# One TensorE-bound decoder trunk: S5 states computed straight from PSUM with one scan per component, and eight projections placed among the quarters of S5's outputs

## The chip, the cores and the metric

The kernel runs on one core of one Trainium2 chip. The metric is the device time of one execution in microseconds (us). Before the change it was 1204.95 us, the median of three runs (1203.24, 1204.95, 1210.08). The engines are named as in the profile: PE is TensorE (PEld its weight loads), DVE is VectorE, ACT is ScalarE, POOL is GpSimd, SP issues the DMAs.

## The reference

Two layers. Each is: half a SwiGLU feed-forward, a mixer, half a SwiGLU feed-forward, all behind RMSNorm, on 272 tokens of width 1024. The change lies in the mixer:

```python
proj = h @ w_in                      # q, k, v | dn_qkv | dn_z | dn_b, dn_a | s5_u
o_sb = rmsnorm(stick_breaking_attention(q, k, v))
o_dn = rmsnorm(gated_deltanet(dn_qkv, b, a)) * silu(z)
bu = einsum(u, b_bar)                # S5, complex, 32 groups x 64 states
states = scan(x_t = abar * x_{t-1} + bu_t)
y = gelu(real(einsum(states, c)) + d * u)
o_s5 = rmsnorm(y * sigmoid(y @ w_glu + b_glu))
out = concatenate(o_sb, o_dn, o_s5) @ w_out
```

## The kernel before

Activations stand transposed in SBUF (128 features of a block by 272 tokens). Each large product is made of three fp32r matmuls (`mm3`: high by high, high by low, low by high), so each weight tile of 128x1024 is first split: ACT rounds it (`wh`, L136) and DVE subtracts (`wl`, L139; six in each mixer go to POOL). A unit (`unit`) is one such tile and 24 matmuls `proj` into one PSUM bank, which DVE empties (L1362 for q, k, v and z).

The mixer of one layer computes in the order of `ORD`. `conv` makes the six blocks of the DeltaNet's qkv. `dn_gates` and `dn_inverse` make the inverse of the triangular matrix of the delta rule: a chain of seven pairs of small DVE steps (L1004, L1005), a transpose T (L1009), and then levels of small matmuls `px` and `py` with a DVE or ACT step between each two. `dn_rest` makes the DeltaNet's outputs.

S5 runs over chunks of four tokens, 68 chunks. Its 16 state pairs are taken as four quarters r of four pairs. `s5` copies u into the chunk layout U, makes the inputs `pinc` (W1 by U) of a quarter in two PSUM banks (real and imaginary part), which ACT copies to `s5z`; then it rotates them (four products with cos and sin, one sum, one difference), runs the scan of each pair and part (8 of 128x68 in a quarter), and rotates back. Two products and one difference of each rotation run on POOL. `s5_outputs` makes the four quarters of outputs `pY` (M0 by U, W2 by the states; 12 fp32 matmuls in a quarter, which the trace shows as 24) and takes their GELU on ACT. `glu` is the gate: `pglu`, tanh, products, and the rounding of the result. `sb` is the attention, from its scores `pz` to its outputs `pob`. `w_out_part` multiplies with the output weights, S5's rows (S) first.

The order on each engine is made by the framework's scheduler, from the priorities in the code (`first()` 4000 for the DeltaNet, `second()` 1500 for the outputs of S5 and the gate) and from the PSUM banks of a tag (two each). `pinc`, `dn_rest` and `pY` share tag b. On an engine, instructions run strictly in their order. An ACT table set (`phase`) stands ahead of the functions that use it.

Of the kernel before, what the change touches and what calls it, by code (L numbers as in the profile page):

```python
# [18 lines left out]
P = 128  # L19
# [21 lines left out]
ORD = "czsrqgbmn"  # L41
# [22 lines left out]
class Trunk:  # L64
    def __init__(self, ctx, tc, a, out):
# [13 lines left out]
        self.blocks = (0, 4)  # L79

# [61 lines left out]
    def mm3(self, p, wh, wl, xh, xl, first, last):  # L142
        mm = self.nc.tensor.matmul
        mm(p, wh, xh, start=first, stop=False)  # L144
        mm(p, wh, xl, start=False, stop=False)  # L145
        mm(p, wl, xh, start=False, stop=last)  # L146
# [126 lines left out]
    def load_params(self, prm):  # L273
# [282 lines left out]
    def s5_alloc(self):  # L556
# [8 lines left out]
        self.dec = c.tile([P, NQ], F32, name="dec")  # L565
# [4 lines left out]
    def s5_tables(self, l, tmp):  # L570
# [17 lines left out]
        pin = tmp.tile([NQ, 3, P], F32, name="pin")  # L588
# [69 lines left out]
        tt(ci, t, rd, ALU.mult)  # L658
        tt(t, e1, e1, ALU.mult)
        tt(self.dec, t, t, ALU.mult)  # L660
# [3 lines left out]
        V.tensor_scalar(r4h, r4, 6144.0, 6144.0, op0=ALU.add, op1=ALU.subtract)  # L664
        tt(r4l, r4, r4h, ALU.subtract)
# [84 lines left out]
        for b in range(2):  # L750
# [20 lines left out]
            for h in range(2):  # L771
# [8 lines left out]
                R0 = tmp.tile([32, 4, P], F32, tag="R0", name="R0", bufs=1)  # L780
# [11 lines left out]
    def s5_tile(self, nm):  # L792
        return self.tmp.tile([P, 4, NCH], F32, tag="s5w", name=nm, bufs=4)

    def s5(self, u):
# [5 lines left out]
        for r in range(4):  # L801
            for j in range(4):
                o = U[32 * (3 - j):32 * (3 - j) + 32, r]
                i = u[32 * r:32 * r + 32].rearrange("p b (c j) -> p b c j", j=4)[:, :, :, j]
                (V.tensor_copy if j % 2 else A.copy)(o, i)  # L805
        self.S = []
        for r in range(4):
            z = []
            for o in range(2):
                p = self.psum("b", "pinc")  # L810
                for b in range(4):
                    PE.matmul(p[:, b * NCH:(b + 1) * NCH], self.W1[o][:, 4 * b + r, :], U[:, r, b, :], start=True, stop=True)
                t = tmp.tile([P, 4, NCH], F32, name=f"s5z{r}{o}")
                A.copy(t, p[:, :T].rearrange("p (b c) -> p b c", b=4))
                z.append(t)
            self.S.append(z)
        for r, z in enumerate(self.S):
            cs, sn = self.cs[:, r::4], self.sn[:, r::4]
            w = [tl("w") for _ in range(4)]
            V.tensor_tensor(w[0], z[0], cs, op=ALU.mult)  # L820
            G.tensor_tensor(w[1], z[1], sn, op=ALU.mult)
            V.tensor_tensor(w[2], z[1], cs, op=ALU.mult)
            V.tensor_tensor(w[3], z[0], sn, op=ALU.mult)
            V.tensor_tensor(z[0], w[0], w[1], op=ALU.add)
            G.tensor_tensor(z[1], w[2], w[3], op=ALU.subtract)
# [14 lines left out]
    def s5_outputs(self, u):  # L840

        A, PE = self.nc.scalar, self.nc.tensor
        for r in range(4):
            p = self.psum("b", "pY")
            for b in range(4):
                q = 4 * b + r
                po = p[:, b * NCH:(b + 1) * NCH]
                PE.matmul(po, self.M0[:, q, :], self.U[:, r, b, :], start=True, stop=False)  # L848
                for k in range(2):
                    PE.matmul(po, self.W2[k][:, q].rearrange("p k g c -> p (k g c)"), self.S[r][k][:, b, :], start=False, stop=k == 1)  # L850
            for t in range(4):
                o = u[32 * r:32 * r + 32].rearrange("p b (c t) -> p b c t", t=4)[:, :, :, t]
                self.act(o, p[32 * t:32 * t + 32, :T].rearrange("p (b c) -> p b c", b=4), AF.Gelu_apprx_tanh)
# [20 lines left out]
    def dn_products(self, rhs, nm, tag):  # L874
# [3 lines left out]
        t, tt = self.dn_tile([P, 8, P], nm), self.dn_tile([P, 32], nm + "t")  # L878
# [13 lines left out]
        return t, tt  # L892

    def dn_gates(self, l, qkv, ba):
# [71 lines left out]
        self.LT, self.LTt = self.dn_products(kb, "LT", "d")  # L966
# [105 lines left out]
    def dn_rest(self, qkv):  # L1072
# [20 lines left out]
        AT, ATt = self.dn_products(qn, "AT", "b")  # L1093
# [88 lines left out]
    def dn_out(self, zg, slot):  # L1182
# [6 lines left out]
        for b in range(2):  # L1189
# [8 lines left out]
            A.activation(self.xh[:, slot + b, :], y, AF.Copy)  # L1198
# [294 lines left out]
```

## Time and profile before

| | |
|---|---|
| median of three runs | 1204.95 us |
| profiled execution, and its span | 1212.91 us, 1211.1 us |
| PE busy | 1172.0 us (97%), mean granted clock 0.955 |
| DVE busy | 866.0 us (72%) |
| ACT busy | 626.1 us (52%) |
| POOL busy | 212.0 us (18%) |

[...] The mixer of layer 0 stands at about 230 to 425 us of the span, that of layer 1 at about 830 to 1030 us.

### The profile page before, as it was taken

The numbers are of one execution on the slowest core, as the hardware profiler recorded it, in microseconds if no ns is written. First come the engines' busy times: TensorE is split into PE (matmuls) and PEld (weight loads), VectorE is DVE, ScalarE is ACT, GpSimd is POOL, SyncE is SP. The second block draws the span as 40 slices with busy tenths as digits, with TensorE's granted clock in tenths as the row PEclk, the third lists the DMA queues.
The fourth block names the chain that finished last, engine by engine and source line by source line (L and its number), as shares of the span: only waits on it lengthen the run. The fifth ranks groups of instructions, "written<-read, shape, count | busy, mean of one in ns | idle before, by whom it ended". The sixth has DMA issues, their size and how long they took to land.

```text
span 1211.1 us, 23894 instructions
## 1 busy us (share of the span) xinstructions
PE 1172.0 (97%) x9544; PEld 1124.1 (93%) x9544; DVE 866.0 (72%) x1680; ACT 626.1 (52%) x995; POOL 212.0 (18%) x256
## 2 busy tenths in 40 slices
PE   8999999998999999999999999999989989999997
PEld 8999999997897999999999999999878969999985
DVE  7999976689626965555579998656994368666644
ACT  6545565473246554444454546645733565555533
POOL 6211111014310111110202112010242001111100
PEclk9999999998669999999999999999986799999999
DMA  6656554533102455555565655455321115666663
GB/s 198 172 168 192 157 155 161 157 105 88 54 18 71 124 173 174 174 175 174 174 184 175 176 168 162 140 175 154 109 88 36 36 52 162 187 184 196 182 191 118
DMA packets 196860, 173.75 MB, mean 143 GB/s; under 512 B 21301, under 2 KB 193005, under 8 KB 196749
## 3 DMA queue, kind: packets, MB, share of 16 engines
q1 hardware_dynamic: 196732, 172.22, 47.1%
q8 instruction: 75, 1.23, 0.4%
q14 instruction: 37, 0.30, 0.1%
q10 hardware_dynamic: 16, 0.00, 0.0%
HBM read 171.15 MB, written 1.05 MB: 142 GB/s over the span
## 4 chain that ended last, share of the span: by engine, by line
PE 84%; DVE 11%; DMA 2%; issue 1%; ACT 1%; POOL 0%; SPq 0%; ACTq 0%; DVEq 0%
PE proj L146 17%; PE proj L144 17%; PE proj L145 17%; PE pd L144 6%; PE pd L146 5%; PE pd L145 5%; PE pd L493 5%; DVE wl L139 2%; PE pY L850 2%; PE pY L848 1%; DVE s5z L829 1%; DVE s5U L805 1%; DVE TT L1005 1%; PE pm L776 1%; PE pw L768 1%
## 5 line engine op out<-in xcount | busy, mean ns | idle before, releaser
L144 PE MATMUL proj<-xh,wh 128*128 128x272 f32 (+1 forms) x1840 | 526.4, 292 | 11.1 <-DVE pq L1362 7.0
L145 PE MATMUL proj<-xl,wh 128*128 128x272 f32 (+1 forms) x1840 | 524.5, 291 | 0.0
L146 PE MATMUL proj<-xh,wl 128*128 128x272 f32 (+1 forms) x1840 | 498.3, 293 | 1.6 <-DVE wl L139 1.2
L139 DVE TENSOR_TENSOR wl<-raw,wh 128x1024 fp32r<-128x1024 f32 (+1 forms) x312 | 380.9, 1221 | 148.7 <-PE pd L146 58.9
L136 ACT ACTIVATE wh<-raw 128x1024 fp32r<-128x1024 f32 (+1 forms) x324 | 338.0, 1044 | 287.4 <-PE proj L145 75.2
L144 PEld LDWEIGHTS proj<-xh,wh 128*128 128x128 f32 x1840 | 350.7, 191 | 15.0 <-DVE pq L1362 7.4
L145 PEld LDWEIGHTS proj<-xl,wh 128*128 128x128 f32 x1840 | 350.4, 190 | 3.1 <-issue 2.0
L146 PEld LDWEIGHTS proj<-xh,wl 128*128 128x128 f32 x1840 | 334.1, 190 | 5.3 <-DVE wl L139 3.3
L435 POOL TENSOR_TENSOR hl<-h,hh 128x272 fp32r<-128x272 f32 (+1 forms) x88 | 81.6, 931 | 463.9 <-ACT hh L434 463.1
L144 PE MATMUL pd<-hh,wh 128*128 128x272 f32 x528 | 150.4, 290 | 0.0
L145 PE MATMUL pd<-hl,wh 128*128 128x272 f32 x528 | 149.4, 288 | 0.0
L146 PE MATMUL pd<-hh,wl 128*128 128x272 f32 x528 | 141.1, 288 | 0.0
L144 PEld LDWEIGHTS pd<-hh,wh 128*128 128x128 f32 x528 | 99.3, 188 | 0.5
L145 PEld LDWEIGHTS pd<-hl,wh 128*128 128x128 f32 x528 | 99.4, 188 | 0.0
L146 PEld LDWEIGHTS pd<-hh,wl 128*128 128x128 f32 x528 | 95.3, 189 | 0.2 <-DVE wl L139 0.2
L107 ACT ACTIVATE g<-g 128x272 f32<-128x272 f32 (+2 forms) x92 | 37.7, 415 | 69.0 <-DVE g L429 68.9
L433 DVE TENSOR_TENSOR h<-proj,g 128x272 f32<-128x272 f32 (+1 forms) x88 | 37.8, 434 | 32.0 <-PE proj L146 19.3
L434 ACT ACTIVATE hh<-h 128x272 fp32r<-128x272 f32 (+1 forms) x88 | 36.3, 419 | 47.0 <-DVE h L433 46.9
L139 POOL TENSOR_TENSOR wl<-raw,wh 128x1024 fp32r<-128x1024 f32 x12 | 28.8, 2397 | 136.0 <-PE proj L146 70.6
L429 DVE TENSOR_TENSOR g<-proj,R 128x272 f32<-128x272 f32 (+1 forms) x88 | 37.5, 431 | 17.3 <-PE proj L146 17.1
L431 DVE TENSOR_TENSOR g<-g,R 128x272 f32<-128x272 f32 (+1 forms) x88 | 38.2, 437 | 14.2 <-ACT g L107 13.9
L376 POOL TENSOR_TENSOR acc<-acc,sq 128x272 f32<-128x272 f32 (+1 forms) x20 | 22.2, 1110 | 89.2 <-ACT sq L370 88.4
(487 smaller groups left out, 1389.2 us busy)
## 6 DMA issues: line engine op xcount, KB each, us to landing
raw<-in_ffn_w_gate_dram SPq DMA_DIRECT2D x88, 512.0 KB, 3.6
raw<-in_ffn_w_up_dram SPq DMA_DIRECT2D x88, 512.0 KB, 3.7
raw<-in_ffn_w_down_dram SPq DMA_DIRECT2D x70, 512.0 KB, 3.5
raw<-in_w_in_dram SPq DMA_DIRECT2D x36, 512.0 KB, 4.3
raw<-in_ffn_w_down_dram SPq DMA_DIRECT2D x24, 384.0 KB, 3.0
raw<-in_w_out_dram SPq DMA_DIRECT2D x16, 512.0 KB, 3.7
raw<-in_s_w_glu_dram SPq DMA_DIRECT2D x4, 512.0 KB, 3.5
xin<-in_x_dram SPq DMA_DIRECT2D x4, 256.0 KB, 5.5
```

The lines of the kernel that those rows point to most:

```text
L107: i = self.nc.scalar.activation(out, in_, func, **k)
L136: nc.scalar.activation(h[:, :n], r[:, :n], AF.Copy)
L139: e.tensor_tensor(l[:, :n], r[:, :n], f32(h[:, :n]), op=ALU.subtract)
L144: mm(p, wh, xh, start=first, stop=False)
L145: mm(p, wh, xl, start=False, stop=False)
L146: mm(p, wl, xh, start=False, stop=last)
L429: V.tensor_tensor(g1, pg[j][:, :N], R, op=ALU.mult)
L431: V.tensor_tensor(g1, g1, R, op=ALU.mult)
L433: V.tensor_tensor(h, pu[j][:, :N], g1, op=ALU.mult)
L434: nc.scalar.activation(hh[:, f, :N], h, AF.Copy)
L435: G.tensor_tensor(hl[:, f, :N], h, f32(hh[:, f, :N]), op=ALU.subtract)
L493: PE.matmul(pd[i][e], x[:, f, ts], w[:, 0, e * 512:e * 512 + 512], start=f == 0 and w is h and x is hh, stop=f == NF - 1 and w is lo)
```

## The change

S5. U is written by `u`'s eviction in a layout with the token within the chunk outermost, so that its copies are contiguous (and `glu` puts the tokens back in order where it rounds). ACT no longer copies `pinc`; DVE multiplies it from PSUM. Real and imaginary part stand in one tile `s5z` of 128x544, so the sum, and each product of the rotation back, is one instruction of 128x544. The decays of the four pairs are laid out as 4x68 with a zero at the first chunk of each pair, so that one scan of 128x272 takes four pairs of one part. POOL keeps only a memset.

Projections. z's and q, k and v's projections left `ORD`; they stand in `do_glu`, one, two, two and three units behind the four quarters of `s5_outputs`. `self.behind` makes the first matmul of the next unit wait in order for the last `pY` of the quarter. z's SiLU became a tanh and a product in the table set of the GELU; the DeltaNet's output gain is applied where `dn_out` rounds. AT overwrites E.

```diff
-ORD = "czsrqgbmn"
+ORD = "csrgbmn"
...
-            for b in range(4):
-                d = self.dec[:, 4 * b + r:4 * b + r + 1].to_broadcast([P, NCH])
-                for o in range(2):
-                    V.tensor_tensor_scan(z[o][:, b, :], d, z[o][:, b, :], 0.0, op0=ALU.mult, op1=ALU.add)
-            w = [tl("w") for _ in range(4)]
-            G.tensor_tensor(w[0], z[0], cs, op=ALU.mult)
-            V.tensor_tensor(w[1], z[1], sn, op=ALU.mult)
...
+            V.tensor_tensor(w[:, 0], pv[0], cs, op=ALU.mult)
+            V.scalar_tensor_tensor(x[:, 1], pv[0], -1.0, sn, op0=ALU.mult, op1=ALU.mult)
+            V.tensor_tensor(w[:, 1], pv[1], cs, op=ALU.mult)
+            V.tensor_tensor(x[:, 0], pv[1], sn, op=ALU.mult)
+            flat = lambda t: t.rearrange("p b c -> p (b c)")
+            V.tensor_tensor(z, w, x, op=ALU.add)
+            for o in range(2):
+                V.tensor_tensor_scan(flat(z[:, o]), flat(dec), flat(z[:, o]), 0.0, op0=ALU.mult, op1=ALU.add)
+
+            w, x = tl("w"), tl("x")
+            V.tensor_tensor(w, z, bc(cs, 1, 2), op=ALU.mult)
+            V.tensor_tensor(x, z, bc(sn, 1, 2), op=ALU.mult)
+            G.memset(z[:, :, :, 0:1], 0.0)
+            V.tensor_tensor(z[:, 0, :, 1:], w[:, 0, :, :-1], x[:, 1, :, :-1], op=ALU.subtract)
+            V.tensor_tensor(z[:, 1, :, 1:], w[:, 1, :, :-1], x[:, 0, :, :-1], op=ALU.add)
...
-                    self.s5_outputs(u)
+                    units = [(proj, 0, q, 0), (proj, 0, q, 1), (proj, 256, k, 0), (proj, 256, k, 1),
+                             (proj, 512, v, 0), (proj, 512, v, 1), (do_z, 0), (do_z, 1)]
+                    for r, n in enumerate((1, 2, 2, 3)):
+                        self.behind = self.s5_outputs(u, r)
+                        for _ in range(n):
+                            f, *args = units.pop(0)
+                            f(*args)
```

On PE, around the inverse's first level in layer 0, the kernel before has units of q, k and v between the small products (`px`, `py` the inverse, `pl` and `pn` products of the DeltaNet, `pinc` S5's inputs):

```order
L144 MATMUL proj<-xh,wh 128x272
L1087 MATMUL pn<-bd_384,sq 128x2 x2
L1089 MATMUL pn<-bd_384,sq 32x1 x2
L1015 MATMUL px<-T_3327,Lm 32x32 x36
L1087 MATMUL pn<-bd_384,sq 128x2 x2
L1089 MATMUL pn<-bd_384,sq 32x1 x2
L886 MATMUL pl<-qkv,kn 128x128 x4
L145 MATMUL proj<-xl,wh 128x272
L146 MATMUL proj<-xh,wl 128x272
```

In the changed kernel the last `proj` of the convolutions is followed there by the small products alone, down to the first output `pY`:

```order
L151 MATMUL proj<-xh,wl 128x272
L826 MATMUL pinc<-s5U,W_588 128x68 x3
L896 MATMUL plt<-kb,kn 32x32 x4
...
L997 MATMUL pl_3302<-r_3300,bd_384 128x512
...
L1093 MATMUL pn<-bd_385,sq 128x2 x2
L1095 MATMUL pn<-bd_385,sq 32x1 x2
L892 MATMUL pl<-qkv,kn 128x128 x8
L896 MATMUL plt<-qkv,kn 32x32 x4
L1021 MATMUL px<-T_3331,Lm 32x32 x36
...
L1027 MATMUL py<-X_3371,TT_3330 32x32 x36
L1116 MATMUL pvt<-ident,qkv 32x64 x4
L854 MATMUL pY<-s5U,M_591 128x68
```

The eight units (192 `proj`) have left this place; nothing of their size has come to it.

At the outputs of S5 the kernel before has on PE the first two quarters one behind the other, with one piece of the inverse between them:

```order
L146 MATMUL proj<-xh,wl 128x272
L144 MATMUL proj<-xh,wh 128x272
L145 MATMUL proj<-xl,wh 128x272
L1021 MATMUL py<-X_3447,TT_3407 32x32 x36
L1108 MATMUL pvt<-ident,qkv 32x64 x4
L848 MATMUL pY<-s5U,M_590 128x68
L850 MATMUL pY<-s5z_3956,W_588 128x68
...
L1032 MATMUL px_3491<-T_3486,LT 32x32 x16
L848 MATMUL pY<-s5U,M_590 128x68
L850 MATMUL pY<-s5z_3970,W_588 128x68
```

The changed kernel has one unit between the first quarter (`s5z_3887`) and the second (`s5z_3914`), and the inverse's second level within them:

```order
L854 MATMUL pY<-s5U,M_591 128x68
L1021 MATMUL px<-T_3410,Lm 32x32 x36
L856 MATMUL pY<-s5z_3887,W_589 128x68
L856 MATMUL pY<-s5z_3887,W_590 128x68
L146 MATMUL proj<-xh,wh 128x272
L150 MATMUL proj<-xl,wh 128x272
...
L1027 MATMUL py<-X_3451,TT_3411 32x32 x36
L150 MATMUL proj<-xl,wh 128x272
...
L854 MATMUL pY<-s5U,M_591 128x68
L856 MATMUL pY<-s5z_3914,W_589 128x68
```

The units now stand behind the outputs, and the outputs behind `pvt`, which is where the DeltaNet gives back the PSUM bank.

On DVE, in S5's second and fourth quarter, the scans stand as follows before (L829, 128x68; the `TT` and `t` rows are the inverse's chain) and now (L837, 128x272):

```order
L829 SCALAR_TENSOR_TENSOR s5z_3970<-dec,s5z_3970 128x68 x2
L829 SCALAR_TENSOR_TENSOR s5z_3977<-dec,s5z_3977 128x68 x3
L1005 TENSOR_TENSOR TT_3309<-TT_3309,t_3310 128x9x4
L829 SCALAR_TENSOR_TENSOR s5z_3977<-dec,s5z_3977 128x68
L1004 TENSOR_TENSOR t_3310<-Lb,TT_3309 128x9x3
L1362 SCALAR_TENSOR_TENSOR pq<-proj,R 128x272
```

```order
L835 TENSOR_TENSOR s5z_3968<-w,x 128x544
L1011 TENSOR_TENSOR TT_3313<-TT_3313,t_3314 128x9x2
L837 SCALAR_TENSOR_TENSOR s5z_3968<-dec,s5z_3968 128x272 x2
L1010 TENSOR_TENSOR t_3314<-Lb,TT_3313 128x9
L1097 TENSOR_SCALAR eq<-pn 128x9
L840 TENSOR_TENSOR w<-s5z_3968,cs 128x544
```

Evictions of units (L1362) stand among the scans before, and none now.

## Rows read from the trace of the kernel before

**Rows 1.** Windows: stretch, length, busy PE, PEld, DVE, ACT, POOL, granted clock, DMA, GB/s.

```profile
264.00:295.50 31.50, 28.75 (x234) 27.30 (x232) 31.00 (x62) 16.27 (x29) 13.90 (x14) 1.00 0.35 98
295.50:309.10 13.60, 10.92 (x186) 10.19 (x187) 12.64 (x33) 0.40 (x1) 6.55 (x12) 0.50 0.26 80
309.10:319.70 10.60, 8.78 (x212) 8.06 (x211) 10.50 (x27) 2.52 (x3) 5.21 (x7) 0.98 0.16 51
319.70:353.60 33.90, 33.90 (x244) 32.91 (x244) 5.02 (x12) 13.47 (x24) 3.18 (x5) 0.50 0.05 17
...
920.30:954.20 33.90, 33.90 (x243) 32.90 (x244) 5.18 (x12) 13.29 (x24) 1.38 (x4) 0.50 0.06 19
...
996.90:1002.00 5.10, 5.10 (x26) 5.10 (x26) 4.43 (x13) 0.88 (x2) 0.00 (x0) 0.50 0.00 0
```

**Rows 2.** Timeline of PE, 265 to 320 us: start, length, instructions, [idle before <-releaser].

```profile
287.80 0.29 PE L144 MATMUL proj<-xh,wh 128*128 128x272 f32 x1
...
288.30 0.29 PE L145 MATMUL proj<-xl,wh 128*128 128x272 f32 x1
...
289.84 1.90 PE L812 MATMUL pinc<-s5U,W 128*128 128x68 f32 x16
291.54 0.37 PE L144 MATMUL proj<-xh,wh 128*128 128x272 f32 x1
...
296.78 0.59 PE L144 MATMUL proj<-xh,wh 128*128 128x272 f32 x1 [3.48 <-DVE pq L1362]
...
300.30 1.19 PE L1015 MATMUL px<-T,Lm 32*32 32x32 f32 x72 [1.40 <-DVE T L1009]
...
319.86 1.06 PE L850 MATMUL pY<-s5z,W 128*128 128x68 f32 x4
320.71 0.63 PE L848 MATMUL pY<-s5U,M 128*128 128x68 f32 x2
```

**Rows 3.** DVE from 267.8 to 319.6 us, by line: busy us, mean ns, idle before.

```profile
L139 DVE TENSOR_TENSOR wl<-raw,wh 128x1024 fp32r<-128x1024 f32 x7 | 9.6, 1378 | 0.0
L829 DVE TENSOR_TENSOR_SCAN s5z<-dec,s5z 128x68 f32<-128x68 f32 x32 | 7.2, 289 | 0.0
L1005 DVE TENSOR_TENSOR TT<-TT,t 128x63 f32<-128x63 f32 (+6 forms) x7 | 4.4, 633 | 0.1
...
L832 DVE TENSOR_TENSOR w<-s5z,sn 128x272 f32<-128x272 f32 x4 | 3.3, 814 | 0.0
L822 DVE TENSOR_TENSOR w<-s5z,cs 128x272 f32<-128x272 f32 x4 | 2.9, 718 | 0.0
L824 DVE TENSOR_TENSOR s5z<-w 128x272 f32<-128x272 f32 x4 | 2.8, 704 | 0.0
L834 DVE TENSOR_TENSOR w<-s5z,sn 128x272 f32<-128x272 f32 x4 | 2.3, 572 | 0.0
L838 DVE TENSOR_TENSOR s5z<-w 128x268 f32<-128x268 f32 x4 | 2.3, 564 | 0.7 <-POOL w L833 0.7
...
L823 DVE TENSOR_TENSOR w<-s5z,sn 128x272 f32<-128x272 f32 x4 | 1.7, 428 | 0.0
...
L1362 DVE SCALAR_TENSOR_TENSOR pz<-proj,R 128x272 f32<-128x272 f32 x2 | 0.9, 428 | 0.0
```

**Rows 4.** DVE before 240 us, by line and shape: a product of 128x544.

```profile
L688 DVE TENSOR_TENSOR cs<-cs,sn 128x544 f32<-128x544 f32 x2 | 1.4, 714 | 0.0
```

**Rows 5.** PE from 319.6 to 353.6 us, by line: busy us, mean ns.

```profile
L850 PE MATMUL pY<-s5z,W 128*128 128x68 f32 x64 | 17.5, 423 | 0.0
```

**Rows 6.** Timelines of ACT, DVE and PE at the gate's end and beyond.

```profile
369.09 1.28 ACT L97 ACT_TABLE_LOAD   x1
...
372.43 0.50 DVE L1292 SCALAR_TENSOR_TENSOR xl<-s5u,prm,xh 128x272 fp32r<-128x272 f32 x1
...
375.47 0.73 PE L388 MATMUL pms<-gacc,ones 128*128 128x272 f32 x2 [0.22 <-DVE gacc L1300]
...
395.56 0.40 PE L144 MATMUL proj<-xh,wh 128*128 128x272 f32 x1 [1.85 <-DVE sy L1433]
```

More of the change, by code (lines that the diff above doesn't have):

```diff
@@ L79, in __init__ @@
         self.blocks = (0, 4)
+        self.behind = None
     def psum(self, tag, nm):
@@ L143, in mm3 @@
         mm = self.nc.tensor.matmul
-        mm(p, wh, xh, start=first, stop=False)
+        i = mm(p, wh, xh, start=first, stop=False)
+        if self.behind is not None:
+            self.order(getattr(i, "ins", i), self.behind)
+            self.behind = None
         mm(p, wh, xl, start=False, stop=False)
@@ L658, in s5_tables @@
         tt(ci, t, rd, ALU.mult)
+        byrow = lambda t: t.rearrange("p (r b) -> p b r", b=4)
+        pairs = lambda t: t.rearrange("p (b r) -> p b r", r=4)
         tt(t, e1, e1, ALU.mult)
-        tt(self.dec, t, t, ALU.mult)
+        d4 = small("d4")
+        tt(byrow(d4), pairs(t), pairs(t), ALU.mult)
+        nc.scalar.copy(self.dec, bc(d4, 2, NCH))
+        G.memset(self.dec[:, :, 0:1], 0.0)
         r4, r4l, r4h = small("r4"), small("r4l"), small("r4h")
@@ L807, in s5 @@
         for r in range(4):
-            z = []
+            z = tmp.tile([P, 2, 4, NCH], F32, name=f"s5z{r}")
+            cs, sn, dec = (t[:, 4 * r:4 * r + 4] for t in (self.cs, self.sn, self.dec))
+            p = []
             for o in range(2):
-                p = self.psum("b", "pinc")
+                p.append(self.psum("b", "pinc"))
                 for b in range(4):
[L812 to L815, printed above, removed]
@@ L840, in s5_outputs @@
[L840 to L853, printed above, removed]
+                    PE.matmul(p[o][:, b * NCH:(b + 1) * NCH], self.W1[o][:, 4 * b + r, :], U[:, r, b, :], start=True, stop=True)
@@ new lines, in s5 @@
+            pv = [t[:, :T].rearrange("p (b c) -> p b c", b=4) for t in p]
+            w, x = tl("w"), tl("x")
[5 more added lines that the diff above has]
+            V.tensor_tensor(z, w, x, op=ALU.add)
@@ new lines, in s5, with s5_outputs @@
+            self.S.append(z)
+    def s5_outputs(self, u, r):
+        PE = self.nc.tensor
+        p = self.psum("b", "pY")
+        for b in range(4):
+            q = 4 * b + r
+            po = p[:, b * NCH:(b + 1) * NCH]
+            PE.matmul(po, self.M0[:, q, :], self.U[:, r, b, :], start=True, stop=False)
+            for k in range(2):
+                i = PE.matmul(po, self.W2[k][:, q].rearrange("p k g c -> p (k g c)"), self.S[r][:, k, b], start=False, stop=k == 1)
+        for t in range(4):
+            o = u[32 * r:32 * r + 32, :, t * NCH:t * NCH + NCH]
+            self.act(o, p[32 * t:32 * t + 32, :T].rearrange("p (b c) -> p b c", b=4), AF.Gelu_apprx_tanh)
+        return getattr(i, "ins", i)
@@ L1092, in dn_rest @@
         qn = qkv[:, 0:2]
[L1093 removed]
+        AT, ATt = self.E, self.Et
+        self.dn_products(qn, AT, ATt, "b")
         vb, kg = [], []
@@ L1355, in mixer, with proj, do_z @@
                 p, = self.unit(w_in[:, 1800 + b * P:1800 + b * P + P], P, "ba"[b % 2])
-                V.tensor_tensor(u[:, b, :], p[:, :T], R, op=ALU.mult)
+                i = lambda t: t.rearrange("p (c j) -> p c j", j=4)
+                V.tensor_tensor(u[:, b, :].rearrange("p (j c) -> p c j", j=4), i(p[:, :T]), i(R), op=ALU.mult)
             zr = tmp.tile([P, 2, T], F32, name="pz")
-            def proj(c0, dst):
-                for b in range(2):
-                    p, = self.unit(w_in[:, c0 + b * P:c0 + b * P + P], P)
-                    V.scalar_tensor_tensor(dst[:, b, :], p[:, :T], 0.125 if c0 == 0 else 1.0, R, op0=ALU.mult, op1=ALU.mult)
+            def proj(c0, dst, b):
+                p, = self.unit(w_in[:, c0 + b * P:c0 + b * P + P], P)
+                V.scalar_tensor_tensor(dst[:, b, :], p[:, :T], 0.125 if c0 == 0 else 1.0, R, op0=ALU.mult, op1=ALU.mult)
             q, k, v = (tmp.tile([P, 2, T], F32, name=f"p{n}") for n in "qkv")
-            def do_z():
-                proj(1536, zr)
-                self.phase(SET_SILU)
-                for b in range(2):
-                    self.act(zr[:, b, :], zr[:, b, :], AF.Silu)
-                    V.tensor_scalar(zr[:, b, :], zr[:, b, :], self.dng[:, l], None, op0=ALU.mult)
+            def do_z(b):
+                proj(1536, zr, b)
+                t = self.cv("zt")[:, :T]
+                self.act(t, zr[:, b, :], AF.Tanh, scale=0.5)
+                V.scalar_tensor_tensor(zr[:, b, :], t, 1.0, zr[:, b, :], op0=ALU.add, op1=ALU.mult)
             def do_s5():
@@ L1379, in do_rest @@
                     self.dn_rest(qkv)
-            def do_qkv():
-                for c0, dst in ((0, q), (256, k), (512, v)):
-                    proj(c0, dst)
             def do_sb():
```

76 lines of the change are left out of this document (30 added, 46 removed).

## The prediction

> **What bounds the kernel now.** I read the windows first, then the timeline of PE in the mixer of layer 0, then DVE's groups in the stretch where PE waits. Outside the mixers PE is busy at full clock, and the change hardly touches that. In a mixer the reader is to see two stretches behind the convolutions [rows 1]. From 264 to 319.7 DVE is busy nearly without a break (31.00 of 31.50 us, 12.64 of 13.60, 10.50 of 10.60), and PE waits for it here and there: 3.48 us for an eviction, after which PE comes back at half clock, and 1.40 us for T [rows 2]. From 319.7 to 353.6 it is the reverse: DVE has 5.02 us of work, and PE is busy all the time at a granted clock of 0.50. What runs there is S5's outputs, and the step of a `pY` matmul is 0.213 us ((320.71 - 319.86) / 4), while `pinc` of the same shape, at clock 1.00, has 0.106 us (1.70 / 16) [rows 2]. L850 alone is 64 matmuls in that stretch [rows 5]; they fill PE, but the clock does not rise from them, since it stays at 0.50 for 33.9 us in both layers [rows 1]. So a mixer loses some 17 us to the clock behind 319.7, more than to waiting.
>
> The change takes the eight units out of the first stretch and lays them into the second. I price both for layer 0; layer 1 has the same stretches (33.90 us at 920.3) and gets the same.
>
> **First stretch: DVE without the units.** From the first S5 product (267.8) to the last of S5 (319.6) DVE needs 51.8 us.
>
> It loses what goes with the units. Five `wl` at 1.378, six evictions, z's two gains and four multiplications and two pieces of the inverse that now stand behind the stretch, fourteen instructions of at most 0.43 [rows 3]: 6.9 + 6.0, less 0.08 of overlap for each of the 19, is 11.4 us.
>
> It loses the collisions with POOL. The products of two SBUF tiles of 128x272 take 0.428 where POOL is quiet (L823), and 0.814, 0.718, 0.704 and 0.572 where it computes beside them; L838 has 0.564 and 0.7 us of waiting [rows 3]. Four of each: 1.5 + 1.2 + 1.1 + 0.6 + 0.5 + 0.7 = 5.6 us. The inverse's L1005 has a mean of 0.633; its operands are no longer than those of a scan of 0.289, so 7 x 0.34 = 2.4 us more. Together 8.0 us. POOL does nothing of S5 afterwards but a memset.
>
> It pays for larger instructions. Before, a quarter is seven products at a step of 0.35 and eight scans at 0.20 (0.289 less the overlap): 4.05 us. Now it is four from PSUM (an eviction, which reads PSUM too, has the same 0.428 as L823, so 0.36 each), three of 128x544 (0.714 [rows 4], 0.62 each), two differences of 0.35 and two scans of 128x272, which no row shows. From below a scan costs what a product of its size does, 0.428; from above what four scans cost one behind the other, 0.80. I take 0.62, nearer the upper end, because the scan of 68 elements is already as long as it is. That is 1.44 + 1.86 + 0.70 + 1.24 = 5.24 us and some 0.2 for results that are used at once: 1.4 us more, 5.6 in four quarters.
>
> [...]
>
> [...]
>
> Sum: 51.8 - 11.4 - 8.0 + 5.6 = 38.0 us. Two products of the DeltaNet stand behind T, 1.3 us, so T is there at 267.8 + 36.7 = 304.5, against 300.3 before [rows 2]. S5 is shorter, but nearly all of it now lies ahead of T. And PE has no `proj` left from about 271 on: the order shows `pinc`, `pl`, `pn` and then `px`, which waits for T. A wait of 3.48 us was enough for half clock [rows 2]; here PE has some 9 us of work in over 30, so it comes to `px` at half clock. The quarters of S5 are ready one by one from about 281, but their outputs stand behind `pvt` in PE's order, so no unit fills the hole.
>
> **Second stretch: PE from T to S5's norm.** Before, PE took 55.9 us from 319.6 to `pms` at 375.5 [rows 6]. Now:
> the outputs and the inverse, at full clock between units, give back 16.5 of the 33.9 us (the smallest matmuls do not double);
> 170 `proj` come in (192 less the 22 of v that were there), at (288.30 - 287.80) / 4 = 0.126 [rows 2]: 21.4 us;
> `px`, `py` twice each and `pv`, which stood ahead of 319.6: 72 matmuls took 1.19 at half clock [rows 2], some 0.75 at full, so 3.9 us with `pv`;
> the clock has to rise first: the first 24 `pY` at 0.213 for 0.106 are 2.6 us, the first 16 `proj` 1.6 and the small products 2.3: 6.5 us;
> at the gate's end a hole. S's first product needs the last block's rounding, which stands on ACT behind the table load (369.09 to `xl` done at 372.9 [rows 6]). Before, the last of the DeltaNet's products covered it; now they are done by then, and only 18 `proj` (2.3 us) do: 2.3 us.
>
> Sum: 55.9 - 16.5 + 21.4 + 3.9 + 6.5 + 2.3 = 73.5 us. `pms` comes at 304.5 + 73.5 = 378.0, 2.5 us later than before. The units' own DVE and ACT work costs nothing: DVE had 5.02 us in 33.9 there. The queue of SP keeps its order, and DMA moved 17 GB/s there.
>
> **The tail.** From 375.5 to the dense run at 395.56 PE waits for the attention's chain, 1.85 us at the end [rows 6] and some 3.7 in all. The DeltaNet is done earlier and three heads' scores are ready together, so I take 1.0 us off. The end moves by +1.5 us in each layer. The first feed-forward has the same work in another buffer order, at nothing: it stands beside dense `proj`.
>
> Against the profiled execution (1212.91 us) that is 1212.91 + 3.0. It lies 8 us above the median of the runs shown, 1204.95, so the forecast is 1204.95 + 3.0 = **1208 us**. Less than 0.5% (6 us) cannot be told from no change.
>
> **The rivals.**
> *No change, as summed* (chance 0.37): 1208, its own range 1199 to 1214.
> *The half clock comes back* (0.35, slower). Place: the second, third and fourth quarters, where 24 `pY` and pieces of the inverse or of the DeltaNet stand for 3 to 4 us without a `proj`, and the gate's hole. For it: `pY` alone never lifted the clock in 33.9 us, and behind a tail with idle PE the clock stood at 0.50 for 5.1 us of dense work [rows 1]. Against: 1.7 us of `pinc` between units did not lower it [rows 2]. Price: 5.1 us at half is 2.5 us, and 1 us for the block itself, 3.5 in all. It decides from one fall in each layer on (+7 us): 1215; with all four, 1208 + 28 = 1236. I take two: 1222.
> *The holes close* (0.28, faster). T comes earlier, if the scans cost what a product does (8 x 0.19 = 1.5 us) and the chain's waits fall between S5's instructions (2 us); the clock rises with the first `pY` and not with the `proj` (2.5); the gate's hole is covered (2.3); the tail's 2.7 us of idle go too. Together 11 us in a layer, 1186; with half of it, 1197, which I take. For it: DVE's sum has the collisions I could only bound. Against: each of the five needs the others' place.
> *It does not do what it says.* The projections are among the quarters in PE's order, but the first quarter itself comes only behind the inverse's first level. That is in the sum.
>
> **Numbers.** Faster by over 0.5% (below 1199): 0.25 from the third and 0.04 from the first's edge, 0.29. Slower (above 1211): 0.31 from the second and 0.05 from the first's edge, 0.36. Within: 0.35. The range leaves out the far ends of the two rivals, a tenth each: 1191 to 1226.
>
> **What would show it.** T's `px` at 302 to 307; from 275 on a granted clock of 0.50 and PE mostly idle until then; the clock at 1.00 from about 318 on; `pY` at 0.106 in the last three quarters; `pms` within 3 us of 378; DVE's scan of 272 between 0.5 and 0.8 us. A clock that falls between 320 and 360, or a PE idle for more than 5 us behind 320, would make it wrong to the slow side; `px` before 300 or a clock at 1.00 before 312 to the fast side.

## The result and the profile after

The changed kernel takes 1214.51 us (median of 13 runs, 1212.50 to 1218.61), the kernel before 1204.47 in the runs beside it (13 runs, 1193.31 to 1213.56): a ratio of 1.011, with a 95% interval of 1.0084 to 1.0137. It is slower, and steadier: 12 of its 13 runs lie within 3 us, while those of the kernel before scatter over 20. (Ratios here compare runs up to 1.5% above a kernel's fastest, so the highest runs of the kernel before are not in them, while medians are of all runs.) The forecast was 1208, with a range of 1191 to 1226: the result lies in the range, on the slow side (above 1211), which had a chance of 0.36.

The executions that were profiled differ by much less: 1214.54 us (span 1212.8) against 1212.91, so +1.6 us. That the medians lie 10 us apart while the profiles lie 1.6 apart is the thing to explain.

The windows of the changed kernel, cut where the clock or the work changes, answer to [rows 1] (stretch, length, busy PE, PEld, DVE, ACT, POOL, granted clock, DMA share, GB/s):

```profile
264.00:271.80 7.80, 7.69 (x71) 7.17 (x69) 7.62 (x14) 3.59 (x8) 2.37 (x1) 1.00 0.49 134
271.80:301.40 29.60, 15.60 (x88) 13.66 (x90) 29.43 (x71) 4.10 (x7) 2.60 (x6) 0.61 0.07 19
301.40:305.00 3.60, 3.60 (x127) 3.21 (x131) 1.76 (x6) 0.40 (x1) 0.00 (x0) 0.50 0.02 5
305.00:368.00 63.00, 62.30 (x790) 58.17 (x778) 25.85 (x52) 26.73 (x54) 8.82 (x7) 1.00 0.26 76
368.00:376.00 8.00, 5.77 (x25) 4.83 (x26) 5.01 (x11) 7.97 (x16) 0.00 (x0) 0.79 0.22 70
397.50:402.50 5.00, 5.00 (x27) 5.00 (x28) 4.96 (x15) 0.73 (x2) 0.00 (x0) 0.66 0.00 0
906.00:970.00 64.00, 63.04 (x795) 58.78 (x787) 27.75 (x54) 28.20 (x56) 6.98 (x6) 1.00 0.26 75
...
971.00:981.00 10.00, 8.77 (x33) 7.63 (x34) 6.85 (x15) 8.99 (x19) 1.22 (x1) 0.50 0.31 93
```

In the 29.6 us ahead of `px` VectorE has hardly a gap (29.43 us busy), and TensorE works for 15.6 us and stands still for 14, at 1.00 only for short spells. From 305 on the clock is 1.00 for 63 us, with 0.7 us of idle time: the 33.9 us at 0.50 of [rows 1] are gone, in layer 1 too. At the gate's end and behind the tail it falls again, to a mean of 0.79 and 0.66, and to 0.50 for 10 us at the gate's end of layer 1.

TensorE's timeline of the same kernel (start, length, instructions, [idle before <-releaser]) answers to [rows 2] and [rows 6]:

```profile
273.95 1.30 PE L826 MATMUL pinc<-s5U,W 128*128 128x68 f32 x8 [2.27 <-DVE L L988]
281.12 2.08 PE L997 MATMUL pl<-r,bd 128*128 128x512 f32 x2 [5.86 <-DVE r L994]
288.77 3.65 PE L826 MATMUL pinc<-s5U,W 128*128 128x68 f32 x16 [2.74 <-DVE TT L1011]
294.85 0.99 PE L1093 MATMUL pn<-bd,sq 128*128 128x2 f32 x4 [2.43 <-DVE TT L1011]
301.36 1.18 PE L1021 MATMUL px<-T,Lm 32*32 32x32 f32 x72
...
305.99 0.61 PE L856 MATMUL pY<-s5z,W 128*128 128x68 f32 x4
...
370.30 0.59 PE L150 MATMUL proj<-xl,wh 128*128 128x272 f32 x1 [1.08 <-DVE xl L1301]
...
375.83 0.62 PE L393 MATMUL pms<-rs,ones 128*128 128x272 f32 x2
...
397.48 0.56 PE L146 MATMUL proj<-xh,wh 128*128 128x272 f32 x1 [2.02 <-DVE sy L1442]
```

Four waits of over 1 us for VectorE, 13.3 us together, stand where [rows 2] had one of 3.48 and one of 1.40. `px` starts at 301.36 against 300.30, S5's `pms` at 375.83 against 375.47, and the dense run at 397.48 against 395.56. These times hold a shift that is not the mixer's: the program's first `pms` is already 1.8 us later here (22.23 against 20.44), and the mixer's first `pc` 1.7 (258.52 against 256.84). Counted from `pc`, `px` comes 0.6 us earlier than before and `pms` 1.3 earlier, and the dense run 0.2 later. And VectorE from 262 to 302 us by line (busy us, mean ns, idle before) answers to [rows 3]:

```profile
L837 DVE TENSOR_TENSOR_SCAN s5z<-dec,s5z 128x272 f32<-128x272 f32 x8 | 5.3, 709 | 0.0
L835 DVE TENSOR_TENSOR s5z<-w,x 128x544 f32<-128x544 f32 x4 | 3.5, 871 | 0.0
L840 DVE TENSOR_TENSOR w<-s5z,cs 128x544 f32<-128x544 f32 x4 | 2.9, 717 | 0.0
...
L830 DVE TENSOR_TENSOR w<-pinc,cs 128x272 f32<-128x272 f32 x4 | 1.8, 440 | 0.1
...
L1011 DVE TENSOR_TENSOR TT<-TT,t 128x63 f32<-128x63 f32 (+6 forms) x7 | 1.3, 190 | 0.0
```

The products cost what was taken (0.440 for one from PSUM, 0.717 for 544 elements), and the inverse's step has fallen from 0.633 to 0.190.

### The profile page after: what moved, and what is told of

It reads as the page before. It is cut to its first block, busy times and chain, and to the rows that moved or that the text cites. A ratio compares the mean times of both kernels' runs of the same rounds, so it can differ in the third digit from the quotient of the medians.

```text
span 1212.8 us, 23751 instructions
## 1 busy us (share of the span) xinstructions
PE 1155.1 (95%) x9544; PEld 1103.4 (91%) x9544; DVE 855.5 (71%) x1649; ACT 614.6 (51%) x981; POOL 174.2 (14%) x210
## 3 DMA queue, kind: packets, MB, share of 16 engines
q1 hardware_dynamic: 196732, 172.22, 47.4%
## 4 chain that ended last, share of the span: by engine, by line
PE 84%; DVE 11%; ACT 3%; issue 1%; DMA 1%; SPq 0%; ACTq 0%; DVEq 0%
PE proj L151 18%; PE proj L150 18%; PE proj L146 18%; PE pd L151 5%; PE pd L150 5%; PE pd L146 5%; PE pd L498 5%; DVE wl L141 2%; PE pY L856 1%; DVE qkv L1351 1%; DVE s5z L837 1%; PE pm L788 1%; PE pz L1247 1%; PE pY L854 1%; DVE s5z L835 1%
```

## The experiments

Two theories at the start. **A, the placement:** units that are taken out of the stretch in which TensorE waits come back in full behind `px`; and the time of the kernel before is a draw, as its half clock does not last equally long in all executions. **B, the new S5:** its work on VectorE is what costs. Layers are compared below from their first `pc` (256.84 and 858.84 in the kernel before) to the first `px`, to S5's `pms` and to the `pms` of the second feed-forward. Each expectation names its own theories by letters; where a result is put beside them, these are meant.

**The kernel before, once more.** No edit.

> The kernel before once more, unchanged, for its own spread: its runs lie between 1193 and 1214 us, those of the changed kernel between 1212.5 and 1218.6. Theory A (the time of the kernel before is a draw: how long its bare pY blocks run at half clock differs from run to run, and the profile of before shows a long draw of 33.9 us in each layer): its runs again scatter by over 8 us, the time falls as the mean granted clock rises, by about 12 us for each 0.01 (33.9 us at 0.50 are 0.014 of the mean clock over 1211 us, and cost 17 us), and a profile with a shorter time shows less of 319.7 to 353.6 or 920.3 to 954.2 at 0.50. Theory B (the scatter comes from loads at the start or elsewhere): the mean clock is the same in all runs within 0.002 while the times scatter.

Median 1202.04. With the 29 runs of the kernel before beside it, the 41 times fall into three groups: 1188.0 to 1193.4 (mean clock 0.967 to 0.975), 1199.8 to 1205.5 (0.960 to 0.966) and 1211.3 to 1214.5 (0.953 to 0.956). Theory A's draw holds: the groups lie 11 us apart, and the longer the time, the lower the mean clock. The new profile, of 1202.0 us, has one layer of each kind (windows of layer 0, then of layer 1; columns as above):

```profile
319.80:333.00 13.20, 13.15 (x191) 12.85 (x191) 3.94 (x9) 9.27 (x16) 1.38 (x4) 0.98 0.13 44
333.00:343.00 10.00, 10.00 (x54) 9.57 (x54) 1.11 (x3) 3.91 (x9) 1.80 (x1) 0.51 0.01 2
909.00:944.00 35.00, 34.78 (x250) 33.82 (x250) 5.96 (x15) 14.06 (x26) 1.39 (x4) 0.51 0.06 20
```

The same instructions in the same order are at half clock for 10 us in layer 0 and for 34 in layer 1. A stretch of 34 us and more at 0.50 is called the long spell below. The layers take 153.5 and 165.8 us to the feed-forward's `pms`. In the profile that the prediction was read from, both are of the long kind (165.5 and 164.8): it shows the highest of the three groups, and the median is the middle one. (No execution of the lowest group was profiled; that neither of its layers has the long spell is taken from the step of 11 us.)

**The new S5 alone.** The units go back to their old places; z has its Silu again, with a factor of two, as the other half of its scale is in `dn_out`.

```diff
-ORD = "csrgbmn"
+ORD = "czsrqgbmn"
...
-                    for r, n in enumerate((1, 2, 2, 3)):
-                        self.behind = self.s5_outputs(u, r)
-                        ...
+                    for r in range(4):
+                        self.s5_outputs(u, r)
```

> The new S5, with the eight units of z, q, k and v back in the places they had before. Theory A (the new S5 is a gain, the placement is the loss): VectorE's stretch loses the collisions (8.0 us) and gains 5.6 us of larger instructions, so px of the inverse comes 1 to 4 us earlier than in the kernel before, counted from the same event; the bare pY blocks run at half clock in a draw as before, so the runs scatter by over 5 us; median 1198 to 1204 us, 3 to 6 below the kernel before at most. Rival (the new S5 itself costs the 10 us, by its VectorE work): about 1214 us or above, and px later than before.

1189.77 us (12 runs, 1188.22 to 1192.00), ratio 0.9948 (0.9916 to 0.998). The new S5 by itself is not what costs: with it and the units in their old places the kernel is 25 us faster than the changed one, which is slow because of the placement. The expectation was wrong on `px` and on the scatter: `px` comes 56 us behind `pc`, not 1 to 4 earlier than before (TensorE's order now has 247 `proj` between the two, where the kernel before has 179), and there is one group of times. Against the lowest group of the kernel before it is no gain; it is one because it seldom draws the long spell. Its windows in layer 0:

```profile
262.00:304.00 42.00, 40.18 (x320) 38.23 (x318) 41.64 (x86) 16.56 (x26) 7.73 (x7) 1.00 0.39 114
304.00:307.00 3.00, 0.56 (x4) 0.22 (x3) 3.00 (x7) 0.87 (x3) 0.00 (x0) 0.99 0.55 183
307.00:324.00 17.00, 16.99 (x292) 14.04 (x292) 9.04 (x20) 1.14 (x4) 0.11 (x1) 0.50 0.10 32
324.00:341.00 17.00, 17.00 (x301) 16.38 (x296) 2.91 (x7) 7.73 (x21) 2.72 (x5) 1.00 0.01 3
```

TensorE's timeline of the same layer:

```profile
257.99 0.28 PE L942 MATMUL pc<-g,triI 128*128 128x8 f32 x2
...
313.99 1.18 PE L1021 MATMUL px<-T,Lm 32*32 32x32 f32 x72
...
361.28 0.62 PE L393 MATMUL pms<-rs,ones 128*128 128x272 f32 x2
```

In the first 42 us TensorE is busy for 40.18, where the changed kernel idles. Then comes a wait, a fall of the clock, and a rise at 324, with bare quarters of S5's outputs behind it at 1.00.

**The old S5 with the units among the quarters.** The kernel before, with the placement of the changed one and nothing of its S5.

> The old S5, with the eight units placed among the quarters of its outputs as in the changed kernel. Theory A (the placement is the loss): TensorE runs dry in the same stretch, VectorE's work there is 51.8 - 11.4 = 40.4 us against the 38 of the changed kernel, so px is 1 to 4 us later than there; the clock is 1.00 through the quarters, so the runs do not scatter (under 4 us); median 1213 to 1220 us. Rival (the placement is free or a gain, the new S5 is the loss): 1204 us or below.

1210.41 (6 runs, 1206.49 to 1212.29), ratio 1.0111 (1.0066 to 1.0157): the whole loss, with the old S5. A holds as to the placement, but not in all of its signs: the time lies 3 us below its range, the runs scatter over 5.8 us, and the clock is at 0.50 for 10 us among the quarters, in both layers (336.0 to 346.3 and 933.3 to 943.6). With this placement the new S5 gains nothing: the changed kernel's lowest run, 1212.50, is above the highest here. Why it loses 4 us there, and gains 12 with the units in their old places, stays open.

**Part of the units ahead of S5.** The changed kernel with four, six or all eight units ahead of S5, and the rest among the quarters.

```diff
+            def do_ahead():
+                for _ in range(4):        # 6, 8
+                    f, *args = units.pop(0)
+                    f(*args)
...
-ORD = "csrgbmn"
+ORD = "cusrgbmn"
...
-                    for r, n in enumerate((1, 2, 2, 3)):
+                    for r, n in enumerate((1, 1, 1, 1)):        # (0, 0, 1, 1), (0, 0, 0, 0)
```

> The changed kernel, with four of the eight units (q and k) ahead of S5, and one unit behind each quarter of the outputs. Theory A (units that run while TensorE waits for VectorE cost only VectorE's share of them): four units are 96 products of 272 columns, 12 us at full clock behind px that go away in each layer, and bring 4 evictions of 0.43 and half of four splits of 1.38 us, some 4.5 us, into VectorE's stretch: 5 to 8 us a layer, if the clock stays at 1.00 in the quarters with 24 products between them; median 1199 to 1207. Rival (one unit for a quarter doesn't hold the clock): 0.50 in the quarters again, scatter over 5 us, 1206 to 1216. Rival (what the hole loses is set by VectorE alone, and the units given back are paid in full in the stretch): 1212 to 1216.

> The changed kernel, with six units (q, k and v) ahead of S5 and only the two of z among the quarters, one behind each of the last two. Theory A (each unit taken out of the stretch in which TensorE waits for VectorE costs the same, whichever it is): all eight among the quarters cost 1214.5 - 1189.8 = 24.7 us against none, four of them 1201.4 - 1189.8 = 11.6, so 1.5 us a unit in each layer; two cost 6: 1194 to 1198 us. Rival (a few units among the quarters keep the clock up and pay for themselves): 1189 us or below. Rival (it is z, whose Tanh and product lie on the chain behind it, that costs): 1202 us or above.

> The changed kernel with all eight units ahead of S5 and none among the quarters; z keeps its Tanh form. Theory A (1.5 us a unit and layer, by the line through eight, four and none among the quarters): 1188 to 1193 us, as the new S5 with the units in their old places. Theory B (bare quarters draw a long spell at half clock): groups of runs 10 us apart, from 1189 up to 1212. Rival (px and the inverse wait behind units and scores on TensorE, as px is put behind them): 1196 to 1204 without scatter.

Four: 1201.40 (1199.59 to 1206.45), ratio 1.0047 (1.0011 to 1.0083), in A's range. Six: 1200.61, ratio 0.9992 (0.9965 to 1.002), in two groups, 1196.2 to 1197.4 in A's range and 1200.4 to 1204.2 above it. Eight: 1223.46 (1221.94 to 1227.19), ratio 1.0236 (1.0187 to 1.0285), slower than the changed kernel and outside all three ranges. So my straight line of 1.5 us a unit has fallen. With all eight ahead the windows of both layers show what came instead:

```profile
262.00:315.00 53.00, 49.85 (x658) 46.15 (x656) 51.84 (x100) 19.40 (x32) 7.56 (x7) 1.00 0.37 111
315.00:369.00 54.00, 51.93 (x361) 49.11 (x362) 12.59 (x36) 12.60 (x32) 4.06 (x7) 0.50 0.00 1
...
915.00:977.00 62.00, 61.56 (x485) 57.18 (x477) 19.42 (x49) 13.16 (x34) 3.56 (x7) 0.50 0.00 1
```

`px` comes 43.5 us behind `pc`, where the changed kernel has 42.8, and the first stretch holds all units at full clock. Then the clock falls (in layer 0 at a wait of 2.04 us for VectorE), and stays at 0.50 for 54 and 62 us although TensorE is nearly always busy. What the placement gained, this spell took back, and more.

**One scan for each pair, and GpSimd's products, in the kernel of 1189.77.**

```diff
-                V.tensor_tensor_scan(flat(z[:, o]), flat(dec), flat(z[:, o]), 0.0, ...)
+                for b in range(4):
+                    V.tensor_tensor_scan(z[:, o, b], dec[:, b], z[:, o, b], 0.0, ...)
```

```diff
-            V.tensor_tensor(w, z, bc(cs, 1, 2), op=ALU.mult)
+            G.tensor_tensor(w, z, bc(cs, 1, 2), op=ALU.mult)
-            V.tensor_tensor(z[:, 0, :, 1:], w[:, 0, :, :-1], x[:, 1, :, :-1], op=ALU.subtract)
+            G.tensor_tensor(z[:, 0, :, 1:], w[:, 0, :, :-1], x[:, 1, :, :-1], op=ALU.subtract)
```

> The new S5 with the units in their old places (the run of 1189.8 us), and its scans cut back into one of 128x68 for each pair: 32 scans instead of 8 in a layer. Theory A (VectorE sets the time of px): 8 scans of 0.708 are 5.7 us, 32 of 0.283 to 0.289 are 9.1 to 9.2: 3.5 us a layer later, 1194 to 1198 us. Rival (VectorE's time there is covered, as TensorE has the units to work on): 1188 to 1192. Rival (the merged scan is what removed the scatter): runs that scatter over 8 us.

> The new S5 with the units in their old places, and two of its operations for each group of four pairs back on GpSimd: the product z*cs behind the scan (128x544) and one of the two differences (128x268), as the old S5 had these on GpSimd. VectorE gives up 4 x (0.72 + 0.43) = 4.6 us a layer. Theory A (collisions cost VectorE about what GpSimd takes over: 20 operations of GpSimd cost 8.0 us in the kernel before): some 3 to 5 us come back as longer VectorE operations, 0.43 as 0.6 to 0.9 in places, and VectorE waits for the product: 1188 to 1194 us. Rival (GpSimd's help is free): 4 to 5 us a layer less, 1180 to 1184. Rival (GpSimd's products of over 2 us on the chain hold the inverse): 1196 us or above, with scatter as in the kernel before.

1211.80, in two groups (1205.1 to 1207.9 and 1215.7 to 1217.0), ratio 1.0014 (0.9976 to 1.0052), and 1220.30 (1217.21 to 1222.42), ratio 1.0156 (1.0131 to 1.0181). These are the times of the last rivals (a scatter of over 8 us, and 1196 or above, though without its scatter), but neither tells a price of its edit: in both, TensorE's order changes too, `px` comes 10 to 12 us earlier, and the spell is long again (the windows of the first, layer 0, then of the second, both layers):

```profile
308.00:362.00 54.00, 54.00 (x429) 50.05 (x425) 13.84 (x40) 11.54 (x31) 3.29 (x6) 0.50 0.01 3
```

```profile
313.00:364.00 51.00, 50.65 (x403) 46.56 (x404) 11.42 (x28) 11.79 (x32) 5.33 (x8) 0.50 0.04 11
917.00:972.00 55.00, 53.84 (x420) 49.77 (x420) 12.51 (x31) 12.59 (x34) 3.53 (x7) 0.50 0.03 11
```

**The kernel of 1189.77 on another chip.**

> The new S5 with the units in their old places once more, unchanged: its 12 runs lay between 1188.2 and 1192.0 us on one chip, while the same kernel with one scan for each pair, run on another chip, lay at 1205 to 1217 in two groups 10 us apart, with 52 us at half clock in its first layer. Theory A (this order of work seldom falls into the long spell at half clock, whatever the chip): 1187 to 1193 us again, all runs. Theory B (how long the spell lasts is a draw for this order too, and the chip weighs it): two or three groups of runs 10 us apart, the lowest at 1189, the others at 1200 and 1211.

1188.86 (12 runs: ten from 1187.73 to 1190.95, two at 1200.51 and 1201.53), ratio 0.9959 (0.992 to 0.9997), on the chip on which its variant with split scans ran. It is faster than the kernel before again, and its two high runs, at a mean clock of 0.961 and 0.962 where the others have 0.972 to 0.977, look like a draw of the long spell (neither was profiled): the expectation's A for most runs, its B for one in six.

**The units behind the last quarter.** The changed kernel with bare quarters; up to `px` nothing differs.

```diff
-                    for r, n in enumerate((1, 2, 2, 3)):
+                    for r, n in enumerate((0, 0, 0, 8)):
```

> The changed kernel, with all eight units behind the last quarter of S5's outputs instead of among them: up to px of the inverse the order is the same, and the same work stands behind it. Theory A (the projections among the quarters hold the clock up): with bare quarters the clock falls to 0.50 for 10 to 34 us somewhere between px and the units, 1219 to 1231 us, with scatter over 5 us. Theory B (the clock comes back at px, and stays whatever stands between the quarters; what costs is only that the units left the first stretch): 1211 to 1217, clock 1.00 from 308 to 360, no scatter.

1214.68 (6 runs: four from 1212.49 to 1215.17 at a mean clock of 0.964 to 0.966, two at 1229.21 and 1229.45 at 0.949 and 0.950). The profile is of the lower group:

```profile
274.00:305.00 31.00, 20.00 (x228) 17.60 (x230) 28.99 (x70) 2.81 (x5) 2.40 (x6) 0.51 0.05 16
305.00:368.00 63.00, 62.10 (x771) 57.94 (x763) 26.49 (x52) 27.38 (x55) 7.93 (x7) 1.00 0.25 77
```

Mostly the expectation's theory B: the projections between the quarters are not what keeps the clock up there. They may guard against a rare fall, since 2 of 6 runs without them lost 15 us and none of 13 with them did; no profile of such a run was taken, so what happens in it stays open.

**One scan for each pair in the changed kernel,** the same edit where VectorE has no gap.

> The changed kernel, with its scans cut back into one of 128x68 for each pair, 32 for 8 in a layer. Theory A (VectorE sets px there, without a gap from 262 to 302): 32 x 0.285 = 9.1 against 8 x 0.71 = 5.7 us of VectorE, so T and px 3.4 us later in each layer and the whole 6 to 8 us: 1219 to 1223 us. Theory B (the merged scan's stretch is covered): 1212 to 1216. Theory C (a part is covered by what the order of TensorE now draws ahead): 1216 to 1219.

1217.90 (6 runs, 1216.61 to 1219.90), +3.4 us. VectorE's row in layer 0:

```profile
L838 DVE TENSOR_TENSOR_SCAN s5z<-dec,s5z 128x68 f32<-128x68 f32 x32 | 7.0, 279 | 0.0
```

7.0 us against 5.3, so 1.7 more in a layer; my 3.4 had added lengths that overlap. The time lies in C's range, but it is not shown to be the price of these scans: `px` comes 0.9 us earlier than in the changed kernel, in both layers (42.0 us behind `pc`). What the profiled run (1219.90, the highest of the six) loses lies behind `px`, 2.6 us in layer 0 and 5.9 in layer 1, where the clock stays at 0.50 for 15.8 us from `px` on, in place of 3.7:

```profile
902.40:918.20 15.80, 15.80 (x351) 14.63 (x351) 6.57 (x16) 1.96 (x5) 1.50 (x5) 0.50 0.01 3
```

**z in the tail.** The changed kernel with z's two units issued behind the gate, and the six others one, one, two and two behind the quarters. They read rows that the gate has overwritten by then, so this z is another one; the work is the same.

> The changed kernel, with the two units of z behind the gate: of their 48 products the last 48 stand behind pms, ahead of the last scores, where TensorE has holes (windows 388 to 404 of the changed kernel: busy 0.67, 0.83, 0.63, and a clock of 0.69 and 0.88 in 396 to 404). Theory A (a unit costs what it takes wherever TensorE has work, and nothing in a hole): the 48 products of 0.125 us, 6.0 us, fill some 3 to 4 us of idle time and keep 1 to 2 us of clock: 3 to 5 us a layer, 1204 to 1209 us. Rival (the price hangs only on what is left in the first stretch): 1212 to 1216. Rival (the attention's scores or dn_out now wait for the units in front of them): 1217 to 1222.

1209.55 (12 runs, 1208.23 to 1214.70), ratio 1.0081 (1.0053 to 1.0108): 5 us less than the changed kernel, just above A's range. The units stand earlier than expected: in the trace z's two are emptied at 365.87 and 368.59 us, and `pms` starts at 365.80, so half or more of their 48 products run ahead of it. In the profile 0.3 us of it lie in layer 0 and 3.6 in layer 1, where 3 to 5 were expected in each. `pms` comes 9 us earlier in both (108.3 behind `pc` in place of 117.3 in layer 0), and all but 0.3 of it is lost again in the tail of layer 0, 5.2 in that of layer 1 (layer 0):

```profile
364.00:376.00 12.00, 10.71 (x81) 9.82 (x79) 7.41 (x16) 9.30 (x18) 2.83 (x2) 1.00 0.40 124
376.00:396.00 20.00, 14.85 (x67) 9.35 (x67) 7.97 (x19) 9.37 (x19) 0.00 (x0) 0.91 0.09 31
```

The units cover the gate's end, where the clock is now 1.00, but the attention's chain sets when the tail is over: its first `pz` of the weights W waits 1.89 us for VectorE and starts 120.3 us behind `pc`, against 120.0 in the changed kernel. In layer 1 the changed kernel has its 10 us at 0.50 at this place, and this one does not.

## Why the prediction was half right

**The sum against the profiled execution came out, but by terms that cancel.** 1212.91 + 3.0 was forecast and 1214.54 measured. From `pc` to the feed-forward's `pms` the layers take +1.3 and +0.8 us, against +1.5. In layer 0, counted from `pc`, `px` is 4.8 us earlier than forecast (the 3.1 below and the shift of 1.7); the second stretch is 1.0 us longer, the tail 2.6 and the dense run behind it 1.0. That they leave 0.2 us is luck. The terms:

- *T and `px`:* 304.5 forecast, 301.36 measured, 3.1 us early. The scans had their price (a step of 0.63 for 0.62), and the products too. The inverse's seven steps fell by 0.44 each for 0.34, 0.7 us in all. Two collisions with the inverse's own products on GpSimd stayed (L835 and L990, below). The other 2 us I can't give to a term.
- *Half clock and idle TensorE from 275 to `px`:* as forecast, with a short rise at 285 to 288.
- *The clock's rise:* at 305.4, at the end of the first `py` and just ahead of the first `pY`, not at 318. The bare quarter behind it ran at 1.00. By the prediction's own signs a clock at 1.00 before 312 spoke for the fast side.
- *Second stretch:* 73.5 forecast, 74.5 measured. The early rise saves part of the 6.5 us set for it; the gate's end takes more than its 2.3, with 2.74 us of waits from 367.86 to 374.50 and the clock at 0.79; some 3 us more are not assigned.
- *The tail:* -1.0 forecast; from `pms` to the dense run it takes 21.65 us against 20.09, so +1.6, and the dense run behind it is 1.0 us longer, as its first 5 us are at a mean of 0.66. The 3.7 us of waits that the prediction read there are 2.9 in the windows (17.08 us busy of 20.00 from 375.5 on in the kernel before).

**The step that failed is the last one, from the profile to the median.** "It lies 8 us above the median of the runs shown, so the forecast is 1204.95 + 3.0" takes the sum over unchanged. But the term of -16.5 us, "give back 16.5 of the 33.9 us", is worth that only in a layer that is at half clock that long. A layer of the short kind ends 12 us earlier (153.5 against 165.8), so a median execution, with one such layer, has that much less to give back. The changed kernel has no such draw: the sum was to be left where it was made, at 1212.91 + 3.0 = 1215.9, 1.4 us from the result (so near by the luck above). The times shown, 1203 to 1210 beside 1212.91 for the profiled execution, should have been asked what their scatter was; I took it as an offset.

**The rivals.** *The half clock comes back* was right in one of its places: not in the quarters, where 305 to 368 is at 1.00, but at the gate's end in both layers (0.50 from 971 to 981 in layer 1). In layer 0 it is at 0.50 from 370.2 to 373.7. It is a fall in each layer, the point at which it was to decide at 1215. Its +7 us is near what the two falls cost by their length (half of 3.4 and of 10.2 us, an estimate), but that 1215 meets the result is luck: it starts from 1208, and the early `px` is not in it. *The holes close:* `px` was early and the clock was up at the first `pY`, as it said; the gate's end and the tail did not close. That the kernel is slower came out as the sum had it, for a reason that the prediction had only in half.

**What the placement does,** then (us, layer 0 / layer 1, from the timelines of the profiles):

| | first `pc` to `px` | to S5's `pms` | to the feed-forward's `pms` | together |
|---|---|---|---|---|
| before, the profile of the prediction | 43.5 / 42.3 | 75.2 / 75.1 | 46.9 / 47.4 | 165.5 / 164.8 |
| before, once more | 42.3 / 43.1 | 64.3 / 75.1 | 46.9 / 47.5 | 153.5 / 165.8 |
| changed | 42.8 / 42.8 | 74.5 / 74.3 | 49.5 / 48.5 | 166.8 / 165.6 |
| new S5, units in their old places | 56.0 / 55.6 | 47.3 / 51.7 | 50.3 / 48.2 | 153.6 / 155.5 |
| old S5, units among the quarters | 47.5 / 46.0 | 70.6 / 67.1 | 49.4 / 47.9 | 167.5 / 161.0 |

The eight units' 192 products at 0.125 us are 24 us, which stand behind `px` now. Against the new S5 with its units in the old places, `px` comes 13 us earlier, and `px` to `pms` takes 74.5 and 74.3 us in place of 47.3 and 51.7. The net at the feed-forward's `pms` is 13.2 and 10.1 us, nearly all of the 25 us between the two. Against the kernel before the same loss is set off by the long spells that it no longer draws: none, one or two of them, some 11 us each.

**Why the long spell does not come here** is shown only as a pattern. The inverse has two pairs of 72-product blocks, each of a `px` and a `py`. In each profiled layer in which the clock fell with a whole pair still to come, it was back at 1.00 by 2.5 us behind the second pair at the latest: at 309 and 910 in the kernel before, at 305 and 906 in the changed one, at 324 in the new S5 alone, at 918 in the changed kernel with split scans. The pair is not needed for it: with the old S5 and the units among the quarters it is back at 302 and 906, ahead of the first `px` (305.5 and 906.7). Where the clock fell later, it stayed at 0.50 for anything from 3 to 61 us. It was 34 us from 319 and 920 in the kernel before, 55 and 61 from 315 and 915 with eight units ahead, and 51 to 55 in three layers of the two variants of the new S5; in these TensorE was busy nearly throughout, and they ended in products of the gate or of projections. But it was 10 us from 333 in the second profile of the kernel before, and 7 and 14 us from 341 and 925 in the new S5 alone. In the changed kernel TensorE's waits lie ahead of the first `px`, and there is none of over 0.1 us from there to 367. What lets a wait of 1.4 to 1.9 us at the same place bring the clock down at once in three layers of the kernel before, for 34 us, and only 13 us later, for 10 us, in the fourth, stays open. That its removal would end the draw was not tried.

## What to carry to other kernels

Before a sum is made against a profiled execution, ask of the run times which of their groups that execution belongs to, and which of its terms only that group has; a second profile of the unchanged kernel answers it. Work that runs while an engine would otherwise wait is cheaper where it is than its own duration says (without the 24 us of the eight units `px` came only 13 us earlier than in the new S5 alone), so moving it to a dense stretch to help the clock must be priced with its full length there. And where the clock is kept by a chance of order, a small edit can shift it by more than the edit's own cost (1188.9 to 1211.8 us on one chip for split scans, which add 3.4 us to the changed kernel): such edits are measured in a kernel whose order they don't change.

## What the runs showed of the hardware

- A TensorE that is busy all the time can stay at 0.50 for long: 54.00 of 54.00 us in the kernel with split scans, 61.56 of 62 with eight units ahead. Most of what it runs there are products of 68 and fewer columns (S5's outputs and the inverse), beside some of 128 and more, and the gate's of 272 at the end. Outputs and inverse, by themselves, run at 1.00 from 324 to 341 in the new S5 alone.
- Scans on VectorE grow with their elements: 0.709 us for 128x272 and 0.279 for 128x68, beside 0.430 us for a product of 128x272. From one scan of 272 to the next it is 0.63 us. The scan of 128x272 takes 1.6 times as long as the product of its size.
- Clock and duration: the 72 products of `px` took 1.18 us at 0.50 and 0.82 at 1.00 (301.36 and 308.09 in the changed kernel), so 1.4 times as long and not twice. The prediction took 0.75 for the latter. The step of a `pY` is 0.11 us at 1.00 ((313.98 - 313.53) / 4 in the changed kernel), beside 0.213 at 0.50 in the kernel before.
- An engine's order: in the kernel before TensorE stood idle for 1.40 us ahead of `px` (300.30), until T was there, though a product of a unit already begun stood behind it. That unit's L144 ran at 297.62, and its next product, L145, which reads the same weights, at 304.56.
- VectorE beside GpSimd: while GpSimd's two products run (2.15 us for both), a VectorE sum of 128x544 takes 1.32 us in place of 0.72, and a product of 128x288 takes 1.04 (VectorE's timeline from 274.22 us, then GpSimd's). In the new S5 alone the same product of 128x288 starts 0.04 us ahead of GpSimd's two (272.94), and takes 0.46 (the last row):

```profile
274.22 1.32 DVE L835 TENSOR_TENSOR s5z<-w,x 128x544 f32<-128x544 f32 x1
275.46 1.04 DVE L990 TENSOR_TENSOR L<-L,m8c 128x288 f32<-128x288 f32 x1
...
283.38 0.72 DVE L835 TENSOR_TENSOR s5z<-w,x 128x544 f32<-128x544 f32 x1
```

```profile
274.04 2.15 POOL L1006 TENSOR_TENSOR Lm<-L,lev 128x288 f32<-128x288 f32 x2 [7.22 <-DVE L L988]
```

```profile
272.90 0.46 DVE L990 TENSOR_TENSOR L<-L,m8c 128x288 f32<-128x288 f32 x1
```
